# Seven-product column pairs for the head projections of a hybrid encoder step, with attention in a stage of its own

## The chip, the core and the metric

The kernel runs on one core of one Trainium2 chip. The metric is device time in microseconds of one execution. The core has five engines that run side by side and wait for each other through semaphores: TensorE (PE; its weight loads are shown as PEld), VectorE (DVE), ScalarE (ACT), GpSimd (POOL) and SyncE (SP). SP does no arithmetic here: it issues DMAs. ACT and POOL issue some too.

## The reference, cut to what matters

One layer of an encoder is applied to two groups of tokens: 512 tokens of a prompt and 8 x 16 tokens of running streams, 640 rows in all. All numbers are float32.

```python
h = rms_norm(x, g_pre)                       # (640, 2048)
parts = split(h @ w_in)                      # (2048, 13312): heads and gates
o_sb = stick_breaking(q, k, v)               # 6 heads of 128, causal
o_bd = band_attention(q, k, v, rel_bias)     # 6 heads, softmax, bias on distance
o_mm = memory_attention(q, mem_k, mem_v)     # 4 heads, 256 memory tokens
merged = sum(sigmoid(merge_gate) * ((o * silu(g)) @ w_up) for the three branches)
y = x + rms_norm(merged @ w_out, g_post)
```

The columns of `w_in` in blocks of 128: queries, keys, values and SiLU gates of the 6 stick-breaking and the 6 band heads (48 blocks), queries and gates of the 4 memory heads (8 blocks), and three merge gates of 2048 columns (48 blocks). The stream tokens attend to cached keys and values of 512 past tokens (256 for memory) in DRAM as well. New keys and values are outputs.

## The kernel before, in words

Everything is held with features on the partitions and the 640 tokens along a row, in two halves of 320. Each float32 operand is split into a high and a low part of a type that TensorE multiplies faster (`split`, L95 to L97: ACT rounds the high part, DVE subtracts to get the low one), and a product is three matmuls: high by high, high by low, low by high. `load_w` (L120) loads a block of weights as `wr` (SP) and `parts_of` (L107) makes `wh` and `wl`.

A **plain block** (`proj`, L152 to L163) is one block of 128 columns: 16 slabs of 128 features x 3 products x 2 halves of tokens = 96 matmuls of 128x320.

A **pair** (`gate_pair`, L674 to L724) takes two blocks of columns at once. It cuts weights and activations into quadrants (two blocks of columns by two halves of the features; two halves of the features by two halves of the tokens) and forms the result of eight quadrant products out of seven, after Strassen and Winograd. Each product is 8 slabs x 3 matmuls, so a pair is 168 matmuls. The weight sums s1 to s4 are made on POOL for each pair. The activation sums t1 to t4 are made once, on DVE and ACT (`sums`, `whole`, `minus`, L616 to L656); t3 is written over b12, a quadrant of the activations.

The order of the program:

1. Memory keys and values, and the normalised activations `xq` (L176 to L278).
2. Twelve causal heads (`causal_head`, L550), stick-breaking and band in turn. Each runs four plain blocks (gate, value, query, key), then the attention of the prompt (`causal_prompt`) and of the streams (`sample_att`), interleaved step by step. Prompt and stream part share one `b` and one `e` buffer.
3. Four memory heads (`mem_head`), each with two plain blocks; then the first four merge gates, plain (`FIRST`, L38), and the sums.
4. The other 44 merge gates as 22 pairs (L726). Each gate is stored to DRAM (`sig_d`) after its sigmoid.
5. `up` (L750): the gated head outputs, read back from DRAM (`osg_d`), times `w_up`, 48 plain blocks of 6 or 4 slabs, summed under the gates into `merged`.
6. The output projection, norm and residual (L781 on).

Cached keys need a transposition. `load_k` (L471 to L477) reads them from DRAM in pieces of 128 bytes, so that DVE can finish it in 32x32 blocks (L486): four DMAs for each two streams and head, 256 in all. The score matmuls of four streams (L490) are sent one after the other; each uses 32 columns of TensorE's array.

The order within each engine is set by the tile framework: a scheduler takes instructions in program order as their priority, with a timeline of its own, and sends a later one ahead where an earlier one isn't ready. A head's attention thus runs between the matmuls of the next head's plain blocks. The queues of the engines themselves are strictly in order.

Of the kernel before, what the change touches and what calls it, by code (L numbers as in the profile page):

```python
# [43 lines left out]
def stream_step_kernel(  # L44
# [10 lines left out]
    KQ = SP  # L55
# [23 lines left out]
    kv_d = dpool.tile([NMEM, 1024], F32, name="kv_d")  # L79
    osg_d = [dpool.tile([P, NT], F32, name=f"osg_d{i}") for i in range(16)]  # L80
    sig_d = [dpool.tile([P, NT], F32, name=f"sig_d{i}") for i in range(3 * KB)]
# [197 lines left out]


    br = ExitStack()
    stg = br.enter_context(tc.tile_pool(name="stg", bufs=3))
# [28 lines left out]
    def head_q(w, col, need_new=True):  # L311
        acc = new_acc()
        proj(w_in, col, KB, x_src, acc)
        qh = pa.tile([P, TP], F32R, tag="qh", name="qh", bufs=B["q"])
        ql = pa.tile([P, TP], F32R, tag="ql", name="ql", bufs=B["q"])
        for d, c in ((slice(0, HF), acc[:, 0, :HF]), (slice(HF, TP), acc[:, 1, :TP - HF])):
            split(qh[:, d], ql[:, d], c)
        qs = acc[:, 1, HF - P:HF]
        qr = None
        if need_new:  # L320
            qr = pa.tile([P, P], F32, tag="qr", name="qr")
            ACT.copy(qr, qs)
        DVE.tensor_copy(masked(qm, 0), qs.rearrange("p (j a i) -> p j a i", j=4, a=2))
        return qh, ql, qr

    def natural_new(src, outs, name):

        ns = pa.tile([P, P], F32, tag=name + "T", name=name + "T")
        POOL.tensor_copy(ns.rearrange("p (a j i) -> p a j i", a=2, i=TS), stream_order(src[:, TP:]))
        new = pa.tile([P, P], F32, tag=name, name=name)  # L330
        t1 = bank("t1")
        PE.transpose(t1[:, :P], ns, ident)
        ACT.copy(new, t1[:, :P])
        POOL.dma_start(outs, new)
        return new, ns

    def head_k(col, outp, outs):
        acc = new_acc()
        proj(w_in, col, KB, x_src, acc)
        kr = pa.tile([P, NT], F32, tag="rawT", name="kr", bufs=B["raw"])  # L340
        ACT.copy(halves(kr), acc[:, :, :HF])
        kh = pa.tile([P, TP], F32R, tag="kh", name="kh", bufs=B["k"])
        kl = pa.tile([P, TP], F32R, tag="kl", name="kl", bufs=B["k"])
        split(kh, kl, kr[:, :TP])

        nat = pa.tile([P, TP], F32, tag="nat", name="natk")
        DVE.transpose(nat, kr[:, :TP])
        for a in range(4):
            KQ.dma_start(outp[:, 32 * a:32 * a + 32].rearrange("(c i) j -> i c j", i=32),
                         nat[32 * a:32 * a + 32].rearrange("p (c j) -> p c j", j=32))  # L350
        _, kn = natural_new(kr, outs, "kn")
        return kn, kh, kl

    def head_v(col, outp, outs):
        acc = new_acc()
        proj(w_in, col, KB, x_src, acc)
        vt = pa.tile([P, NT], F32, tag="rawT", name="vt", bufs=B["raw"])
        ACT.copy(halves(vt), acc[:, :, :HF])
        nat = pa.tile([P, 4, P], F32, tag="nat", name="nat")
        t0 = bank("t0")  # L360
        for t in range(4):
            PE.transpose(t0[:, t * P:(t + 1) * P], vt[:, t * P:(t + 1) * P], ident)
        DVE.tensor_copy(nat, t0.rearrange("p (t n) -> p t n", t=4))
        POOL.dma_start(outp.rearrange("(t p) e -> p t e", p=P), nat)
        vn, _ = natural_new(vt, outs, "vn")
        vh = pa.tile([P, 4, P], F32R, tag="vh", name="vh", bufs=B["v"])
        vl = pa.tile([P, 4, P], F32R, tag="vl", name="vl", bufs=B["v"])
        split(vh, vl, nat)
        return vn, vh, vl

    def head_g(col):
        acc = new_acc()
        proj(w_in, col, KB, x_src, acc)
        sg = pa.tile([P, NT], F32, tag="sg", name="sg", bufs=B["sg"])
        ACT.activation(halves(sg), acc[:, :, :HF], AF.Sigmoid)
        DVE.tensor_tensor(halves(sg), acc[:, :, :HF], halves(sg), op=ALU.mult)
        return sg

    def w_tiles():
        return (pa.tile([P, 1024], F32R, tag="wth", name="wth", bufs=B["wt"]), pa.tile([P, 1024], F32R, tag="wtl", name="wtl", bufs=B["wt"]))  # L380

    def causal_prompt(q, k, v, sg, kind, strip):

        qh, ql, kh, kl, vh, vl = *q, *k, *v
        for pair in (1, 0):
            nkb = 2 * pair + 2
            wth, wtl = (t.rearrange("p (k n) -> p k n", n=256) for t in w_tiles())
            POOL.memset(wth[:, nkb - 1, 0:P].bitcast(F32), 0.0)
            POOL.memset(wtl[:, nkb - 1, 0:P].bitcast(F32), 0.0)
            for ql_ in (1, 0):  # L390
# [6 lines left out]
                b = pa.tile([P, NT], F32, tag="b", name="b", bufs=B["b"])  # L397
                if kind == "sb":
                    e = pa.tile([P, NT], F32, tag="e", name="e", bufs=B["e"])
# [40 lines left out]
    def mem_prompt_att(q, k, v, sg):  # L440
        qh, ql, kh, kl, vh, vl = *q, *k, *v
        wth, wtl = (t.rearrange("p (k n) -> p k n", n=512) for t in w_tiles())
# [17 lines left out]
    def sample_att(ck, cv, qr, kr, vn, sg, kind, strips):  # L460
        nkb = ck.shape[1] // P
# [9 lines left out]
        def load_k(b):  # L471

            t = pa.tile([P, 2 * nc_ // 32, 32], F32, tag="kc", name="kc", bufs=B["kc"])
            for a in range(4):
                SP.dma_start(t[32 * a:32 * a + 32],
                             ck[b:b + 2, :, 32 * a:32 * a + 32].rearrange("b (c j) i -> j (b c) i", j=32))
            return t.rearrange("p c i -> p (c i)")  # L477

        s = bank("s")
        for par in range(2):  # L480
            kts = []
            for j in range(0, 4, 2):
                kc = load_k(4 * par + j)
                for h in range(2):
                    kt = pa.tile([P, nc_], F32, tag="kt", name="kt", bufs=B["kt"])
                    DVE.transpose(kt, kc[:, h * nc_:(h + 1) * nc_])  # L486
                    kts.append(kt)
                    yield
            for j in range(4):
                PE.matmul(s[32 * j:32 * j + 32, :nc_], qm[:, j, par * 32:par * 32 + 32], kts[j],  # L490
                          start=par == 0, stop=par == 1, tile_position=(0, 32 * j))
            yield
        b = pa.tile([P, NT if new else nc_], F32, tag="b", name="b", bufs=B["b"])
        if new:
            s2 = bank("s2")
            PE.matmul(s2[:, :P], qr, kr, start=True, stop=True)
        if kind == "sb":
            e = pa.tile([P, NT], F32, tag="e", name="e", bufs=B["e"])
# [15 lines left out]
        tp = bank("tp")  # L514
# [3 lines left out]
        o = bank("o")  # L518
        if new:
            t2 = bank("t2")  # L520
# [19 lines left out]
        t3 = bank("t3")  # L540
# [3 lines left out]
    def spill(osg, i):  # L544
        POOL.dma_start(osg_d[i], osg)

    def tokens(t):
# [313 lines left out]
```

## Time and profile before

| | |
|---|---|
| median of 3 runs | 2223.4 us (2222.37 to 2224.03) |
| profiled execution | 2225.07 us, its span 2223.4 us |
| mean granted clock of TensorE | 0.984 |
| stage of the heads and first gates | 95 to 1183 us |
| stage of the gate pairs | 1183 to 1749 us |
| `up` | 1749 to 1985 us |
| output projection | 1985 to 2223 us |

A profile line names the source line (L162), the engine, the operation, the output and inputs by the program's names (`acc<-xh,wh`), the shape and the count (x1920); after the bar stand busy time in us, mean duration in ns, and the idle time of that engine just before, with what ended it. A wait reads "A <- B": A waited for B. "wr<-in_w_in_dram" is a DMA, "SPq" its issue on SP. In the table by stage each engine has its busy time and, in brackets, its count of instructions; then come the granted clock, the busy share of the 16 DMA engines and GB/s.

### The profile page before, as it was taken

How to read it: one execution, taken by the hardware profiler on the slowest of the kernel's cores; microseconds unless marked ns; L12 is line 12 of the kernel's file. 1: busy time of each engine (PE TensorE's matmuls, PEld its weight loads, DVE VectorE, ACT ScalarE, POOL GpSimd, SP SyncE). 2: the span in 40 equal slices, each digit the busy share in tenths (PEclk: the TensorE clock that was granted, in tenths of full speed). 3: DMA queues.
4: the chain of work that ended last, by engine and by line, in shares of the span. 5: the costliest groups of instructions: out<-in, count | busy, mean ns of one | idle time of the engine just before them, and what ended most of it. 6: DMA issues, size and time to landing. Idle time of an engine off the chain costs nothing.

```text
span 2223.4 us, 36183 instructions
## 1 busy us (share of the span) xinstructions
PE 2147.6 (97%) x14277; PEld 1992.9 (90%) x14277; DVE 1074.8 (48%) x1795; ACT 789.0 (35%) x1484; POOL 423.1 (19%) x443
## 2 busy tenths in 40 slices
PE   6999999999999999999997999999999999999997
PEld 4899899898988999978986999999999899998886
DVE  7624444444444444438438555555555434582224
ACT  6422333333323333224344444444444312232221
POOL 3100010000100100000003444544544002340000
PEclk8999999999999999999999999999999999999998
DMA  7665556555564646525442433343333545443224
GB/s 232 181 152 117 133 130 150 128 129 138 146 148 99 155 130 151 144 71 132 124 109 71 132 117 100 104 131 115 100 107 113 161 143 167 145 152 110 76 85 161
DMA packets 574006, 288.55 MB, mean 130 GB/s; under 512 B 277488, under 2 KB 537600, under 8 KB 572812
## 3 DMA queue, kind: packets, MB, share of 16 engines
q1 hardware_dynamic: 560748, 253.18, 43.1%
q10 hardware_dynamic: 9216, 19.93, 2.3%
q0 software_dynamic: 3872, 13.13, 1.7%
q8 instruction: 112, 1.84, 0.3%
q14 instruction: 58, 0.48, 0.1%
HBM read 249.97 MB, written 36.19 MB: 129 GB/s over the span
## 4 chain that ended last, share of the span: by engine, by line
PE 75%; issue 13%; DVE 5%; DMA 3%; POOL 2%; SPq 1%; ACT 1%; ACTq 0%; DVEq 0%; POOLq 0%
PE acc L162 33%; PE q L687 23%; PE ya L148 3%; PE ya L150 3%; PE ya L149 3%; PE s L490 3%; DVE wl L97 2%; POOL merged L764 1%; PE o L535 1%; DMA sig<-sig_d 1%; DMA st<-rext_d 1%; PE tp L413 1%; PE acc L149 0%; PE o L149 0%; DVE yt L828 0%
## 5 line engine op out<-in xcount | busy, mean ns | idle before, releaser
L97 DVE TENSOR_TENSOR wl<-wr,wh 128x512 fp32r<-128x512 f32 (+1 forms) x548 | 411.2, 753 | 621.6 <-ACT wh L96 618.6
L96 ACT CAST wh<-wr 128x512 fp32r<-128x512 f32 (+1 forms) x548 | 330.5, 607 | 806.8 <-PE acc L162 463.6
L162 PE MATMUL acc<-xl,wh 128*128 128x320 f32 x1920 | 453.7, 312 | 0.0
L162 PE MATMUL acc<-xh,wh 128*128 128x320 f32 x1920 | 447.5, 312 | 4.7 <-ACT sig L633 2.5
L162 PE MATMUL acc<-xh,wl 128*128 128x320 f32 x1920 | 450.5, 312 | 0.0
L162 PEld LDWEIGHTS acc<-xh,wh 128*128 128x128 f32 x1920 | 323.8, 189 | 25.0 <-issue 18.6
L162 PEld LDWEIGHTS acc<-xh,wl 128*128 128x128 f32 x1920 | 324.3, 189 | 18.0 <-issue 18.0
L162 PEld LDWEIGHTS acc<-xl,wh 128*128 128x128 f32 x1920 | 325.8, 189 | 15.4 <-issue 14.7
L687 PE MATMUL q<-xh,wh 128*128 128x320 f32 x704 | 218.3, 311 | 5.1 <-ACT wh L96 5.1
L97 DVE TENSOR_TENSOR wl<-ws,wh 128x512 fp32r<-128x512 f32 x176 | 154.6, 879 | 140.1 <-ACT wh L96 139.9
L687 PE MATMUL q<-xh,wl 128*128 128x320 f32 x704 | 214.8, 310 | 5.8 <-DVE wl L97 5.8
L687 PE MATMUL q<-xl,wh 128*128 128x320 f32 x704 | 218.0, 310 | 0.0
L687 PE MATMUL q<-th,wh 128*128 128x320 f32 x528 | 163.2, 309 | 0.7 <-DVE sig L697 0.7
L687 PE MATMUL q<-th,wl 128*128 128x320 f32 x528 | 163.2, 309 | 0.0
L687 PE MATMUL q<-tl,wh 128*128 128x320 f32 x528 | 163.1, 309 | 0.0
L96 ACT CAST wh<-ws 128x512 fp32r<-128x512 f32 x176 | 109.1, 621 | 151.8 <-PE q L687 151.8
L687 PEld LDWEIGHTS q<-xh,wh 128*128 128x128 f32 x704 | 133.1, 189 | 5.6 <-ACT wh L96 5.6
L687 PEld LDWEIGHTS q<-xh,wl 128*128 128x128 f32 x704 | 132.0, 189 | 6.7 <-DVE wl L97 6.7
L687 PEld LDWEIGHTS q<-xl,wh 128*128 128x128 f32 x704 | 133.1, 189 | 0.0
L148 PE MATMUL ya<-wh,gh 128*128 128x512 f32 x320 | 126.6, 396 | 1.0 <-DVE sig L763 1.0
L150 PE MATMUL ya<-wh,gl 128*128 128x512 f32 x320 | 126.6, 395 | 0.0
L149 PE MATMUL ya<-wl,gh 128*128 128x512 f32 x320 | 126.6, 395 | 0.0
(204 smaller groups left out, 3100.9 us busy)
## 6 DMA issues: line engine op xcount, KB each, us to landing
wr<-in_w_in_dram SPq DMA_DIRECT2D x208, 512.0 KB, 4.5
wr<-in_w_out_dram SPq DMA_DIRECT2D x32, 512.0 KB, 3.7
sig_d<-sig ACTq DMA_DIRECT2D x48, 320.0 KB, 3.4
sig<-sig_d SPq DMA_DIRECT2D x48, 320.0 KB, 3.4
kc<-in_cache_sb_k_dram SPq DMA_DIRECT2D x96, 128.0 KB, 3.2
vc<-in_cache_sb_v_dram SPq DMA_DIRECT2D x48, 256.0 KB, 5.8
kc<-in_cache_band_k_dram SPq DMA_DIRECT2D x96, 128.0 KB, 3.2
vc<-in_cache_band_v_dram SPq DMA_DIRECT2D x48, 256.0 KB, 5.1
```

What stands on the lines that cost most here:

```text
L96: ACT.copy(hi, src)
L97: DVE.tensor_tensor(lo, src, hi.bitcast(F32), op=ALU.subtract)
L148: PE.matmul(out, ah, bh, start=start, stop=False)
L149: PE.matmul(out, ah, bl, start=False, stop=False)
L150: PE.matmul(out, al, bh, start=False, stop=stop)
L162: PE.matmul(acc[:, s, :HF], a[:, k], b[s], start=first and f, stop=last and l)
L413: PE.transpose(tp[:, kb * P:(kb + 1) * P], b[:, kb * P:(kb + 1) * P], ident)
L490: PE.matmul(s[32 * j:32 * j + 32, :nc_], qm[:, j, par * 32:par * 32 + 32], kts[j], start=par == 0, stop=par == 1, tile_position=(0, 32 * j))
L535: PE.matmul(o[32 * j:32 * j + 32, :P], l, r, start=i == 0, stop=i == len(steps) - 1, tile_position=(0, 32 * j))
L687: PE.matmul(bank_, a[:, k], b[:, k], start=first and k == 0 and n == 0, stop=k == KH - 1 and n == 2, skip_group_check=not first)
L764: POOL.tensor_tensor(merged[:, j], merged[:, j], sig, op=ALU.add)
```

## The change

All 56 head blocks become 28 pairs. They run, with ten pairs of merge gates, in a stage ahead of attention, and their results go to DRAM: SiLU gates to `sg_d`, queries, keys and values to `q_d`, `k_d`, `v_d` as high and low parts with the stream columns beside them. Four merge gates stay plain at the start (`FIRST`), with the sums beside them. Attention is a later stage: each head loads its parts from DRAM; a head's stream part is interleaved with the next head's prompt part; and 24 merge gates (`LAST`) are plain blocks beside it, traced behind the head of each round, so with a lower priority than that head and a higher one than the next. The quadrant b12 is kept in DRAM and loaded again before that stage.

The cached keys are rearranged by DMAs from DRAM to DRAM (`cut_keys`), 256 of 128-byte pieces, seven behind the weight loads of each pair on SP. Attention then loads them whole, one DMA for each stream. The score matmuls go out two by two, with three `kt` buffers instead of four, six `vc` buffers instead of eight, two `b` and two `e` buffers for the prompt, and `bs` and `es` of its own for the stream part. PSUM is divided anew: eight banks for the pairs; three for late gates, two for stream parts and three for prompt parts in attention.

In `up`, one more buffer holds head outputs, and the split of `merged` is traced within the third branch.

```diff
-B = dict(wr=3, wh=4, wl=4, kc=2, kt=4, vc=8, sg=3, b=1, e=1, raw=1, q=1, k=1, v=1, wt=1)
+B = dict(wr=3, wh=4, wl=4, kc=3, kt=3, vc=6, sg=3, b=2, q=2, v=1, wt=1, nat=1)
 FIRST = 4
+LAST = 24
...
+    def sums(k):
+        r = stg.tile([P, NT], F32, tag="o", name="r")
+        r0, r1 = r[:, :HF], r[:, HF:]
+        r2 = flat()[:, :HF]
+        whole(b11, k, r0), whole(b12, k, r1), whole(b22, k, r2)
+        minus(t1, k, r1, r0)
+        minus(t2, k, r2, r0)
+        minus(t4, k, whole(b21, k, r1), r0)
+    for i in range(FIRST):
+        gate(i)
+        for k in range(KH * i // FIRST, KH * (i + 1) // FIRST):
+            sums(k)
+    def sums3():
+        for k in range(KH):
+            r = stg.tile([P, NT], F32, tag="o", name="r")
+            minus(t3, k, whole(b22, k, r[:, :HF]), whole(b12, k, r[:, HF:]))
...
     def load_quads(col):
...
+        with tc.issue_after(last.ins if hasattr(last, "ins") else last):
+            cut_keys(7)
...
+    def two_parts(o, to):
+        h = flat()
+        split(h.bitcast(F32R), o.bitcast(F32R), o)
+        ACT.dma_start(to[0], h)
+        SP.dma_start(to[1], o)
...
+    class Keys(Queries):
+        def done(self, o, q):
+            nat = flat()
+            DVE.transpose(nat, o[:, :TP])
+            for a in range(4):
+                SP.dma_start(self.outp[:, 32 * a:32 * a + 32].rearrange("(c i) j -> i c j", i=32),
+                             nat[32 * a:32 * a + 32].rearrange("p (c j) -> p c j", j=32))
+            ns, _ = natural_new(o, self.outs)
+            ACT.dma_start(self.to[2], ns)
+            two_parts(o[:, :TP], self.to)
...
+    def cut_keys(n):
+        for to, src, a in cuts[:n]:
+            SP.dma_start(to[32 * a:32 * a + 32].rearrange("p (c i) -> p c i", i=32),
+                         src[:, :, 32 * a:32 * a + 32].rearrange("b (c j) i -> j (b c) i", j=32))
+        del cuts[:n]
...
+    for n, job in enumerate(jobs):
+        block_pair(*job, *([sums3] if n == 0 else []))
+    gs.close()
+    psb.close()
+    for t, d in zip(b12, b12_d):
+        SP.dma_start(t.bitcast(F32), d)
...
-            for j in range(0, 4, 2):
-                kc = load_k(4 * par + j)
-                for h in range(2):
+            for j0 in range(0, 4, 2):
+                kts = []
+                for j in (j0, j0 + 1):
+                    st = 4 * par + j
+                    kc = pa.tile([P, nc_], F32, tag="kc", name="kc", bufs=B["kc"])
+                    SP.dma_start(kc, kx[st // 2][:, st % 2 * nc_:(st % 2 + 1) * nc_])
                     kt = pa.tile([P, nc_], F32, tag="kt", name="kt", bufs=B["kt"])
-                    DVE.transpose(kt, kc[:, h * nc_:(h + 1) * nc_])
+                    DVE.transpose(kt, kc)
                     kts.append(kt)
-                    yield
-            for j in range(4):
-                PE.matmul(s[32 * j:32 * j + 32, :nc_], qm[:, j, par * 32:par * 32 + 32], kts[j],
-                          start=par == 0, stop=par == 1, tile_position=(0, 32 * j))
-            yield
+                for j, kt in zip((j0, j0 + 1), kts):
+                    PE.matmul(s[32 * j:32 * j + 32, :nc_], qm[:, j, par * 32:par * 32 + 32], kt,
+                              start=par == 0, stop=par == 1, tile_position=(0, 32 * j))
+                yield
...
+    heads = [("mm", h) for h in range(4)] + [("sb", h) for h in range(6)] + [("bd", h) for h in range(6)]
     with tc.tile_pool(name="att", bufs=1, reuse_waits="tile") as pa:
         qm, wTm = zero_padded(4)
...
+        before = ()
+        for i, (kind, h) in enumerate(heads + [(None, None)]):
+            mark = last_on_pe()
+            now = mem_head(h) if kind == "mm" else causal_head(h + 6 * (kind == "bd")) if kind else ()
+            interleave(*now[:1], *before)
+            before = now[1:]
+            with tc.issue_after(mark):
+                for n in range(LAST * i // 17, LAST * (i + 1) // 17):
+                    late_gate(3 * KB - LAST + n)
```

`block_pair` is `gate_pair` for any pair of columns: its ends are objects (`Gate`, `Silu`, `Queries`, `Keys`, `Values`) that finish the two results and store them. `late_gate` is `gate` with the two halves of tokens in banks of their own, the second half of the features first.

More of the change, by code (lines that the diff above doesn't have):

```diff
@@ L326, in natural_new @@
[L326 to L369, printed above, removed]
@@ L767, in stream_step_kernel @@
         up(i)
[L768 to L770 removed]
+        if i >= 2 * KB:
+            j = i % KB
+            split(gh[:, j], gl[:, j], merged[:, j])
     br.close()
[L772 removed]
+    psd.close()
     py = ctx.enter_context(tc.tile_pool(name="py", bufs=1, reuse_waits="tile"))
```

438 lines of the change are left out of this document (253 added, 185 removed).

## The prediction

> **What bounds the kernel now.** I read the page's busy times first.
>
> ```profile
> span 2223.4 us, 36183 instructions
> PE 2147.6 (97%) x14277; PEld 1992.9 (90%) x14277; DVE 1074.8 (48%) x1795; ACT 789.0 (35%) x1484; POOL 423.1 (19%) x443
> PE 75%; issue 13%; DVE 5%; DMA 3%; POOL 2%; SPq 1%; ACT 1%; ACTq 0%; DVEq 0%; POOLq 0%
> PE acc L162 33%; PE q L687 23%; PE ya L148 3%; PE ya L150 3%; PE ya L149 3%; PE s L490 3%; DVE wl L97 2%; POOL merged L764 1%; PE o L535 1%; DMA sig<-sig_d 1%; DMA st<-rext_d 1%; PE tp L413 1%; PE acc L149 0%; PE o L149 0%; DVE yt L828 0%
> ```
>
> TensorE is busy for 97% of the span, the next engine for 48%. The chain that ended last (rows three and four) is 75% PE and 13% issue, over half of it projections (L162 plain, L687 in pairs). So the time is a count of matmuls times their pace, plus the places where PE waits. Busy time by stage, cut where the first matmul of each stage starts, says where those are.
>
> ```profile
> core 0: us, PE busy (x) PEld busy (x) DVE busy (x) ACT busy (x) POOL busy (x), PEclk, DMA share, GB/s
> 0.00:95.00 95.00, 68.17 (x304) 53.74 (x305) 73.44 (x125) 55.11 (x100) 27.58 (x19) 0.87 0.64 205
> 95.00:1183.00 1088.00, 1074.92 (x7742) 984.27 (x7740) 491.49 (x965) 361.95 (x707) 71.90 (x207) 0.99 0.54 131
> 1183.00:1749.00 566.00, 549.53 (x3740) 546.12 (x3739) 309.56 (x413) 256.28 (x461) 259.58 (x177) 0.99 0.34 110
> 1749.00:1985.00 236.00, 230.73 (x1536) 228.10 (x1536) 124.57 (x158) 63.14 (x110) 58.14 (x31) 0.99 0.54 163
> 1985.00:2223.40 238.40, 224.22 (x960) 180.65 (x960) 75.72 (x138) 52.56 (x107) 5.90 (x9) 0.98 0.35 111
> ```
>
> The second row is the heads (56 plain blocks, all attention, four gates), the third the 22 gate pairs. PE is idle for 1088.0 - 1074.9 = 13.1 us in the one and 566.0 - 549.5 = 16.5 us in the other: 29.6 us. Busy isn't pace, so the pace comes from a stretch of pairs and from successive rows of a plain block in the timeline.
>
> ```profile
> 1300.00:1700.00 400.00, 400.00 (x2729) 400.00 (x2728) 212.38 (x276) 181.52 (x324) 185.36 (x128) 1.00 0.36 115
> 309.27 0.45 PE L162 MATMUL acc<-xh,wh 128*128 128x320 f32 x2
> 309.56 0.46 PE L162 MATMUL acc<-xl,wh 128*128 128x320 f32 x2
> 309.86 0.46 PE L162 MATMUL acc<-xh,wl 128*128 128x320 f32 x2
> ```
>
> 2729 matmuls in 400 us is 0.1466 us each, so a pair of 168 takes 24.6 us. Plain rows hold two and start 0.29 or 0.30 us apart: the same pace. A pair saves only by its count: two plain blocks are 192 matmuls. The 60 plain blocks of the head stage are 60 x 96 x 0.1466 = 844 us. Of its 1088 us, 244 us are left: 13 idle, 231 for attention's matmuls and transposes.
>
> **The change part by part.** *Products.* The heads' 56 blocks become 28 pairs, four gates stay plain, ten gate pairs remain, and 24 gates go back from pairs to plain blocks. Pairs rise from 22 to 38, plain blocks fall from 60 to 28: 16 x 24 = 384 matmuls fewer, **-56.3 us**. With the two old stages their idle time goes, **-29.6 us**; what stands in its place is costed now.
>
> *First four gates with the sums.* They are 56.3 us of PE. Beside them run the sums of eight slabs, ten DVE instructions each, priced by the first row here, and 16 weight subtractions by the second.
>
> ```profile
> L619 DVE TENSOR_TENSOR r<-xh,xl 128x320 f32<-128x320 f32 x41 | 19.3, 482 | 0.3
> L97 DVE TENSOR_TENSOR wl<-wr,wh 128x512 fp32r<-128x512 f32 x239 | 165.2, 692 | 330.8 <-ACT wh L96 329.8 <-PE acc L162 0.9
> L97 DVE TENSOR_TENSOR wl<-ws,wh 128x512 fp32r<-128x512 f32 x129 | 113.3, 878 | 107.5 <-ACT wh L96 107.3
> 1190.46 4.65 DMA osg_d<-sg
> or<-osg_d SPq DMA_DIRECT2D x16, 320.0 KB, 3.4
> ```
>
> 80 x 0.482 + 16 x 0.692 = 49.7 us: it fits, with 88% of DVE taken. Between 0 and 6 us of waiting; I take 3. *First pair.* The third operand is made in place, in b12, after the last plain gate has read it: 8 x 4 x 0.482 = 15.4 us of DVE, beside ten weight subtractions of the first five products, 8 us by the second and third row. That is 23.5 us against 5 x 24 x 0.1466 = 17.6 us of matmuls: **+6**. Nothing hides the rest, as PE has no other work there.
>
> *Other engines in the pair stage.* A pair now holds 212.4 x 24.6 / 400 = 13.1 us of DVE. A pair of key heads adds two 128x512 transposes and two subtractions, under 3 us by the 692 ns row: 16 of 24.6, still beside matmuls. The value and new-token transposes on PE move here from the head stage; none is added.
>
> *Key caches.* 256 DMAs leave the head stage; 256 DRAM-to-DRAM ones, with both sides in 128-byte pieces, join the pairs, seven behind each pair's last weight load on SP. These are rows on such pieces: the 128-byte reads (kc), 128-byte stores to DRAM (natk), the queue's share in the heads (400 to 900 us), and 5 us with four natk stores.
>
> ```profile
> L475 SPq DMA_DIRECT2D kc<-in_cache_sb_k_dram x96: 311/642/2050, 98.5 to 847.6; - x96
> kc<-in_cache_sb_k_dram SPq DMA_DIRECT2D x96, 128.0 KB, 3.2
> out_dram<-natk SPq DMA_DIRECT2D x48, 64.0 KB, 3.6
> q1 hardware_dynamic: 224127, 62.87, 54.6%
> 232.70:237.70 5.00, 5.00 (x35) 4.86 (x34) 1.95 (x4) 0.89 (x2) 0.54 (x1) 1.00 0.74 170
> DMA packets 3175, 0.85 MB, mean 170 GB/s; under 512 B 2135, under 2 KB 3159, under 8 KB 3175
> ```
>
> SP spends 7 x 0.642 = 4.5 us per pair on issuing. Behind them wait the next pair's weight loads, needed up to 24.6 us later: covered. On the 16 DMA engines a packet of the heads took 0.546 x 500 x 16 / 224127 = 19.5 ns on average. In the last two rows, 0.74 x 5 x 16 us over 2135 small packets is at most 27.7 ns. Nothing in the trace reads and writes such pieces in one transfer, so the cost lies between 0 and the sum of two such packets; I take 19.5 ns, the row with most of them. The 229,376 pieces are then 280 us of the engines' time. The pairs themselves have 0.36 x 936 = 337 us, and the stores of 28 head pairs, about 1.1 MB at 115/0.36 GB/s, 98 us. Together 715 us in a stage of 38 x 24.6 = 936 us: hidden, **0**. The Trainium skill ("DMA: Bandwidth & Descriptors", Specifications) speaks against this: below 512 B the engine does a read-modify-write. The natk row fits that, taking 3.6 us for half the bytes that kc lands in 3.2; a doubling by that rule is the second rival.
>
> *Change into attention.* Its pool takes over the pairs' memory, so head 0's loads wait for the last pair's stores: the last two rows of the fence above the key caches, 4.65 + 3.4 = **+8**, without the first late gate as cover; with it, 0 to 3.
>
> *Attention.* PE has 24 x 96 x 0.1466 = 338 us of gates and 231 us of attention less some 6 us of moved transposes: 563 us, 35 us per head. DVE keeps at most 491.5 - 165.2 = 326 us and gets 96 x 0.692 = 66 for the gates: 393 of 563, not the bound. The cached-key scores go out in twos, no longer in fours:
>
> ```profile
> L490 PE MATMUL s<-kt,qm 128*32 128x512 f32 (+1 forms) x256 | 81.7, 551 | 0.0
> 326.46 1.06 PE L490 MATMUL s<-kt,qm 128*32 128x512 f32 x8
> 972.76 1.05 PE L490 MATMUL s<-kt,qm 128*32 128x512 f32 x4
> 978.25 1.05 PE L490 MATMUL s<-kt,qm 128*32 128x512 f32 x2
> ```
>
> One matmul is two records. One alone takes as long as two or four together, as they share the array. The 82 us now lie between all in fours and all alone. In twos throughout it is about 21 us less; all alone, 34 us more (96 x 1.05 plus 32 half-length ones, less 82). I take **0**, as the present mix already comes from a scheduler that sends each when its key tile is ready. The stage's idle time: the heads' 13.1 us, or 2.5 times it (33) if waiting grows as filler falls from 60 blocks to 24. I take **+20**. Up and output projection stay as they are.
>
> Sum: -56.3 - 29.6 + 3 + 6 + 8 + 20 = **-48.9 us**. The profiled execution took 2225.07 us, 1.7 more than its span; the median of runs equals the span, 2223.4. Forecast: **2174 us**.
>
> **Rivals.** *Attention's own pace sets the end.* A head is a chain of scores, stick or softmax, transposes, values, through four engines. In the trace, the last causal head (its first and last score block, its end) and the last memory head ran with the least beside them:
>
> ```profile
> 953.61 0.48 PE L148 MATMUL s<-kh,qh 128*128 128x512 f32 x1
> 986.65 0.36 PE L148 MATMUL s<-kh,qh 128*128 128x256 f32 x1
> 999.68 0.47 PE L541 MATMUL t<-ident,on 128*128 128x128 f32 x1 [0.39 <-ACT on L538]
> 1152.71 0.28 PE L148 MATMUL s<-kh,qh 128*128 128x256 f32 x1
> 1189.51 0.33 PE L541 MATMUL t<-ident,on 128*128 128x128 f32 x1 [0.41 <-ACT on L538]
> 986.60:1000.40 13.80, 10.00 (x105) 7.81 (x103) 5.32 (x16) 4.17 (x10) 0.00 (x0) 0.75 0.28 71
> ```
>
> 46.1 us and 36.8 us. If nothing overlaps, 12 x 46.1 + 4 x 36.8 = 700 us instead of 583: 2291, slower than before. It decides from (583 + 49)/16 = 39.5 us per head. For it: the granted clock fell to 0.75 where filler was missing. The Trainium skill ("TensorE: Matmul & The Clock Gate", Why this matters for your kernels) has the clock halved after some 3 us of idle PE; the row agrees. Against it: those heads shared one b and one e buffer between prompt and sample part. The change gives the prompt two, the sample its own, and runs a head's sample beside the next head's prompt. The parts are 33 and 13 us, so the longer alone gives 35 or less. 0.09.
>
> *DMA becomes the bound of the pairs.* At twice 19.5 ns the pieces take 559 us, with the rest 994 us against 936: +58, 2232, slower. It decides from 35 ns. For it the natk row; against it that reading and writing of one piece may overlap. 0.05.
>
> *The gates are used up early.* They rank ahead of later heads, so fillers can run out. With five heads left bare, each at half of 46.1 us (two overlapped) instead of the 14 us of PE that it needs: +45, 2219, no change that can be told. It decides when filler is spent at twice the even rate. 0.06.
>
> **How the numbers follow.** The forecast has 0.80. Its own range: without attention's waiting and with scores in twos (-20 - 21), and nothing at first gates, first pair and changeover except 3 (-14), 2119; with 33 us of waiting and scores alone (+13 + 34), 2221. The range given drops the extreme of the low end, where all bounds fall together, and reaches to the third rival and just past 2223: 2126 to 2226. A measurement of this kernel tells about 0.2%, 4.4 us, from no change. Faster: 0.79 of the forecast and 0.02 of the third rival, 0.81; same: 0.01 + 0.04 = 0.05; slower: the first two rivals, 0.14.
>
> **What would show it.** Right: pairs at 24.6 us each from the second on, 38 of them in about 945 us; a PE chain with few DMA steps in that stage; attention at about 583 us with PE over 95% busy; x2 and x4 score rows mixed as now. Wrong: pairs longer than 25 us with PE waiting for wr loads (second rival); PE idle in attention with ACT, DVE or POOL as releaser and a clock under 0.95 (first); no L162-like gate rows in the last heads (third). The forecast is wrong altogether if attention's PE work isn't near 225 us.

## The result, and the profile after

The changed kernel takes 2287.6 us (median of four runs, 2283.17 to 2292.57) against 2223.7 us for the kernel before in the same session: a ratio of 1.028, interval 1.0253 to 1.0311. It is slower by 64 us, where 49 us less had been forecast. The profiled execution took 2292.57 us, with a mean granted clock of 0.975. Busy times and the chain that ended last, from the page of the changed kernel:

```profile
span 2290.9 us, 36585 instructions
PE 2144.2 (94%) x13893; PEld 1950.5 (85%) x13893; DVE 1241.3 (54%) x1919; ACT 862.9 (38%) x1641; POOL 613.3 (27%) x533
PE 78%; DMA 10%; DVE 6%; issue 2%; ACT 2%; SPq 1%; ACTq 0%; POOL 0%; DVEq 0%; POOLq 0%
PE qa L470 19%; PE g L829 14%; PE acc L167 12%; PE qc L470 9%; PE qb L470 4%; DVE wl L102 3%; PE s L710 3%; PE ya L155 3%; PE ya L153 3%; PE ya L154 3%; PE o L755 2%; DMA kc<-kx 2%; DMA wr<-in_w_in_dram 2%; DMA out_dram<-nat 1%; ACT wh L101 1%
```

The matmuls did go: 14277 - 13893 = 384 fewer, as counted. Yet PE's busy time fell by only 3.4 us: those that were left took longer in sum, at a mean granted clock of 0.975 where it was 0.984, and PE's share of the span fell from 97% to 94%. In the chain DMA has grown to 10% (3% before); the line in which DVE makes the low part of the weights (L102, before L97) has 3%, where it had 2%. The table by stage (before the first gates, first gates with sums, pairs, attention, `up`, output projection) shows where:

```profile
0.00:95.00 95.00, 67.46 (x302) 52.94 (x303) 73.25 (x124) 54.71 (x100) 27.50 (x19) 0.93 0.67 213
95.00:152.00 57.00, 57.00 (x389) 56.82 (x388) 42.62 (x78) 21.50 (x41) 10.10 (x8) 1.00 0.62 193
152.00:1176.00 1024.00, 973.58 (x6462) 954.17 (x6462) 623.41 (x782) 438.31 (x819) 467.54 (x326) 0.99 0.57 148
1176.00:1820.00 644.00, 593.94 (x4250) 479.05 (x4249) 299.86 (x640) 232.12 (x466) 43.52 (x139) 0.95 0.67 208
1820.00:2055.00 235.00, 230.74 (x1549) 229.18 (x1550) 128.13 (x160) 63.64 (x111) 60.25 (x33) 0.99 0.53 161
2055.00:2290.90 235.90, 221.46 (x950) 178.35 (x948) 74.05 (x137) 52.60 (x107) 4.37 (x9) 0.98 0.35 112
```

The forecast had 936 + 6 us for the pairs and 8 + 583 for attention. They took 1024 and 644: 82 and 53 us more. The last two stages took 471 us against 474 before. PE was idle for 50 us in each of the two new stages, where 26 had been allowed in both together.

**The pairs.** Pace shows best in a count of the products' matmuls alone. Below are those of the source line that issues them, in a stretch of causal heads (320 to 920 us) and one of gate pairs (980 to 1120 us). Columns: PE and PEld busy with counts, granted clock, DMA share, GB/s.

```profile
320.00:920.00 600.00, 557.78 (x3678) 543.99 (x3679) 0.99 0.63 159
980.00:1120.00 140.00, 139.67 (x949) 138.96 (x948) 1.00 0.55 138
```

With 168 matmuls in a pair, 600 x 168 / 3678 = 27.4 us in the heads and 140 x 168 / 949 = 24.8 us in the gates. So the pace forecast, 24.6, holds for gate pairs, with cache pieces beside them, and fails by some 2.7 us on average for the pairs of the causal heads. It isn't every kind of result: the last two of the four pairs of the memory heads, which end in SiLU gates and queries but have no keys or values, took 49.9 us together (217.8 to 267.7 us). In the timeline, the 24 pairs of the causal heads and the pair behind them, in which the last one's results are finished, ran from 267.7 to 951.8 us: 684 us instead of 616, **+68**. The waits from 320 to 950 us, each with its total, how often, and its longest:

```profile
DVE wl L102 <- ACT wh L101: 148.8, 154, 4.7
DVE o L102 <- DMA out_dram<-o: 56.7, 11, 6.6
ACT nat L101 <- DMA out_dram<-nat: 19.4, 8, 4.0
PEld qa L470 <- DVE wl L102: 18.5, 21, 1.8
PEld qa L470 <- ACT wh L101: 14.6, 13, 2.2
PEld t L452 <- ACT o L413: 7.2, 6, 1.5
PEld tn L427 <- POOL ns L425: 5.6, 12, 1.1
```

Read from the bottom up. PE waits for parts of the weights (rows four and five) and for its own transposes of results (six and seven). DVE, which makes the weights' low parts, has stood up to 6.6 us at `o`: the low part of a result is written over `o`, and must wait until the store of `o` to the output has landed. ACT, which makes the high parts, stands in the same way at `nat`, a single buffer. DVE has 16.5 us of work in each of these pairs (380.2 us from 320 to 950 us, in 630 / 27.4 = 23 pairs), close to the 16 forecast for pairs of keys. It isn't short of time; its queue is in order, and weight parts stand behind a result's store. The first row isn't a sign of loss: the same wait is longer in the faster runs e1 and e7 (253 and 262 us). Three rows of the timeline, behind one pair of keys, show both engines held: ACT behind a store, DVE until ACT's first cast in that row was done (the view names a load that landed in the same moment), and then DVE by a store (in brackets the idle time before, and what ended it):

```profile
482.93 1.14 ACT L101 CAST wh<-wr 128x512 fp32r<-128x512 f32 x2 [3.70 <-DMA out_dram<-new]
483.58 1.29 DVE L102 TENSOR_TENSOR wl<-wr,wh 128x512 fp32r<-128x512 f32 x2 [3.63 <-DMA wr<-in_w_in_dram]
490.94 0.71 DVE L440 STREAM_TRANSPOSE nat<-o 128x512 f32<-128x512 f32 x1 [2.57 <-DMA kh_d<-nat]
```

**The first pair** (the first 168 matmuls of the products) took 40.7 us, 16 over 24.6, where 6 had been allowed; its clock fell to 0.83. **Attention** falls into a part while late gates last, and a bare end:

```profile
1176.00:1714.00 538.00, 531.11 (x3774) 440.57 (x3773) 254.87 (x532) 210.66 (x413) 38.35 (x121) 0.99 0.69 214
1714.00:1820.00 106.00, 62.83 (x476) 38.47 (x476) 44.98 (x108) 21.46 (x54) 5.17 (x18) 0.74 0.57 177
```

While there are gates, 7 us are lost in 538. Then the last three and a half heads run alone, some 30 us each: 43 us idle in 106, and what runs has a granted clock of 0.74. The longest wait of SP's queue there, for a buffer of cached values (L695) held by the value matmuls (L755):

```profile
SPq L695 <- PE o L755: 25.1, 7, 15.1
```

### The profile page after: what moved, and what is told of

The parts are those of the page before. It is cut to its first block, busy times and chain, and to the rows that moved or that the text cites. A ratio compares the mean times of both kernels' runs of the same rounds, so it can differ in the third digit from the quotient of the medians.

```text
span 2290.9 us, 36585 instructions
## 1 busy us (share of the span) xinstructions
PE 2144.2 (94%) x13893; PEld 1950.5 (85%) x13893; DVE 1241.3 (54%) x1919; ACT 862.9 (38%) x1641; POOL 613.3 (27%) x533
## 4 chain that ended last, share of the span: by engine, by line
PE 78%; DMA 10%; DVE 6%; issue 2%; ACT 2%; SPq 1%; ACTq 0%; POOL 0%; DVEq 0%; POOLq 0%
PE qa L470 19%; PE g L829 14%; PE acc L167 12%; PE qc L470 9%; PE qb L470 4%; DVE wl L102 3%; PE s L710 3%; PE ya L155 3%; PE ya L153 3%; PE ya L154 3%; PE o L755 2%; DMA kc<-kx 2%; DMA wr<-in_w_in_dram 2%; DMA out_dram<-nat 1%; ACT wh L101 1%
## 5 line engine op out<-in xcount | busy, mean ns | idle before, releaser
L102 DVE TENSOR_TENSOR wl<-wr,wh 128x512 fp32r<-128x512 f32 (+1 forms) x516 | 395.5, 771 | 430.1 <-ACT wh L101 418.6
L102 DVE TENSOR_TENSOR wl<-ws,wh 128x512 fp32r<-128x512 f32 x304 | 317.2, 1058 | 131.1 <-ACT wh L101 129.0
L829 PE MATMUL g<-xh,wl 128*128 128x320 f32 x768 | 242.4, 316 | 0.0
L829 PE MATMUL g<-xl,wh 128*128 128x320 f32 x768 | 242.1, 315 | 0.0
L829 PE MATMUL g<-xh,wh 128*128 128x320 f32 x768 | 241.1, 314 | 0.0
L470 PE MATMUL qa<-xh,wh 128*128 128x320 f32 x608 | 193.6, 318 | 13.7 <-ACT wh L101 9.5
L470 PE MATMUL qa<-xh,wl 128*128 128x320 f32 x608 | 193.5, 318 | 12.2 <-DVE wl L102 11.8
L470 PE MATMUL qa<-th,wh 128*128 128x320 f32 x608 | 189.0, 311 | 7.2 <-DVE o L474 5.7
L463 POOL TENSOR_TENSOR ws<-wr 128x512 f32<-128x512 f32 x114 | 167.8, 1486 | 98.1 <-DVE wl L102 62.0
L470 PE MATMUL qa<-xl,wh 128*128 128x320 f32 x608 | 190.8, 314 | 2.6 <-DVE xl L102 2.6
L470 PE MATMUL qa<-th,wl 128*128 128x320 f32 x608 | 188.2, 309 | 1.8 <-DVE wl L102 1.8
L470 PE MATMUL qa<-tl,wh 128*128 128x320 f32 x608 | 187.8, 309 | 0.0
```

Of the source, the lines that this page charges most:

```text
L102: DVE.tensor_tensor(lo, src, hi.bitcast(F32), op=ALU.subtract)
L463: eng.tensor_tensor(o, a[c], b[c], op=op)
L470: PE.matmul(bank_, a[:, k], b[:, k], start=first and k == 0 and n == 0, stop=k == KH - 1 and n == 2, skip_group_check=not first)
L829: PE.matmul(acc[s], a[:, k], b[s], start=(k0, k, n) == (8, 0, 0), stop=(k0, k, n) == (0, 7, 2))
```

## The experiments

The texts on record give the theories letters. A: the store of each result in two parts holds DVE and ACT up, and weight parts behind them. B: the cache pieces slow the landings. C: late gates are sent too early and leave the last heads bare. D: heads have a pace of their own, and gates beside them are free. E: the lost time is the place of a pair's end work in the queues, whether it waits for landings or not. G: SP's queue stands at buffers and keeps loads back. Medians go against the kernel before on the same chip, 2226.0 to 2228.3 us. Where no interval is given, the kernel ran once.

**e1_raw** stores each result whole and splits it after loading, in attention (A).

```diff
     def two_parts(o, to):
-        h = flat()
-        split(h.bitcast(F32R), o.bitcast(F32R), o)
-        ACT.dma_start(to[0], h)
         SP.dma_start(to[1], o)
...
-        for to, src in zip(t, d):
+        for to, src in list(zip(t, d))[1:]:
             SP.dma_start(to.bitcast(F32), src)
+        split(t[0], t[1], t[1].bitcast(F32))
```

> Queries, keys and values go to DRAM whole, and each head splits them when it loads them in the attention stage; nothing is split, and nothing is overwritten in place, at the end of a head pair. Theory A (DVE and ACT stand in order behind the landings of result stores, with the weight parts of the next products queued behind them): the head pairs fall from about 27.3 us to 25.3 or less, 25 of them, so the pair stage loses 50 us or more; attention gains 33 us of DVE work spread over 642 us and stays within 10 us; total about 2240. Theory B (the key-cache pieces crowd the weight loads out of the DMA engines): the pairs stay at about 27, total within 10 us of 2288.

It took 2257.4 us, ratio 1.014 (1.0125 to 1.0155). The products' matmuls from 320 to 920 us:

```profile
320.00:920.00 600.00, 571.53 (x3820) 562.21 (x3820) 1.00 0.60 149
```

That is 26.4 us per pair: 1.0 us of the 2.7, neither A's 25.3 nor B's 27. DVE's wait at `o` is gone, and PE's waits for weight parts are down from 33 us to 10.5; those at the transposes of new tokens have grown from 5.6 to 10.4. The waits for landings that are left lie at other results (PE's rows first):

```profile
PEld qa L467 <- DVE wl L102: 5.3, 10, 1.0
PEld qa L467 <- ACT wh L101: 5.2, 8, 1.0
PEld tn L424 <- POOL ns L422: 10.4, 12, 2.1
POOL ns L422 <- DMA ks_d<-ns: 33.8, 6, 6.2
ACT wh L101 <- PE tn L424: 30.9, 6, 5.7
```

POOL now stands at the new tokens' buffer, PE's transpose waits for POOL, and ACT, which is to copy its result, has a weight part queued behind it. A is right in kind and a third of the size.

**e2_nocuts** leaves the rearrangement of the caches out (B); attention loads plain rows instead.

```diff
-        with tc.issue_after(last.ins if hasattr(last, "ins") else last):
-            cut_keys(7)
...
-                    SP.dma_start(kc, kx[st // 2][:, st % 2 * nc_:(st % 2 + 1) * nc_])
+                    SP.dma_start(kc, kx(st, nc_))
```

> The rearranging DMAs are left out; attention loads rows of the same size from the caches as they lie, so its cached keys are not the right ones and the cached scores are meaningless. Theory B (key-cache pieces crowd out the weight loads): head pairs fall from 27.3 us to about 24.6, total about 2220. Theory A (in-order waits for landings of result stores): head pairs stay between 26.5 and 27.5, total within 20 us of 2288.

It took 2260.7 us. The same stretch, and the wait at `o`:

```profile
320.00:920.00 600.00, 577.19 (x3869) 567.83 (x3869) 1.00 0.44 135
DVE o L102 <- DMA out_dram<-o: 39.1, 9, 6.2
```

26.1 us per pair, 1.3 better, with a shorter wait at the same place. So the copies, costed at 0, cost about a microsecond in each head pair, though the DMA engines were busy for 63% of that stretch, and next to nothing in gate pairs, which store little. They did not crowd out the weight loads, as B had it: those landed in 5.2 us at the median with the copies and without. Most stores landed sooner without them (those of `o` to the output in 4.4 us for 4.8, of `nat` in 3.0 for 4.1), two of ACT's later (`qh_d` and `vh_d`).

**e8_raw_nocuts** does both.

> Parts stored whole, and the rearranging DMAs left out as well (cached keys not the right ones). Each of the two alone took 0.9 and 1.2 us off a head pair of 27.3. If they are two ways into the same loss (a queue waits for a store to land, and landings take longer beside the key-cache pieces), both together give little more than the better one: about 25.8. If they are separate losses they add up: about 25.2, and the rest is PE's own waiting for transposes.

It took 2257.0 us, as e1 alone:

```profile
320.00:920.00 600.00, 572.10 (x3838) 563.25 (x3838) 1.00 0.39 116
```

26.3 us per pair. A and B don't add: with the parts' stores gone the copies cost nothing (26.4 with, 26.3 without). They are two handles on one loss: copies lengthen the landings at which DVE and ACT stand, as most of the medians above have it. The copies also hold SP's queue, 0.757 us each at the median, with stores behind them; the runs don't part this from the longer landings.

**e5_defer** traces the whole end of a pair (transposes, splits, stores) behind the second product of the next pair.

```diff
-        e0.done(o0, SP)
...
-        e1.done(o1, ACT)
+        late_ends.extend([lambda: e0.done(o0, SP), lambda: e1.done(o1, ACT)])
...
         product(qb, a12, b21, True)
         add(o0[:, LO], qb)
+        finish()
```

> The end work of a pair (transposes, splits, stores of its two results) is traced behind the second product of the next pair instead of at the end of its own, so that it comes after that pair's first weight parts and PE meets its transposes when their inputs are long there. Nothing else changes. Theory E (the lost time is the end work's place in the in-order queues of PE, ACT and DVE): head pairs fall from 27.3 us to 25.3 or less, pair stage about 970, total about 2235. Theory A in its first form (only the waits for store landings count, wherever the end work stands): DVE still stops for each landing with weight parts behind it, pairs stay at 26.5 or more, total 2270 or more.

It took 2278.8 us, ratio 1.0235 (1.0218 to 1.0252), at 26.8 us per pair:

```profile
320.00:920.00 600.00, 571.78 (x3757) 561.84 (x3756) 0.98 0.64 163
```

PE's waits at its transposes are gone; that was about 0.6 us a pair. The waits for weight parts moved with the end work, as A had it and not E: pairs now alternate between 24.6 to 25.0 us (behind SiLU gates and queries) and 27 to 31 (behind values and keys).

**e3_pin** holds each round's late gates back until the previous round's attention (C).

```diff
-        before = ()
+        before, mark = (), last_on_pe()
         for i, (kind, h) in enumerate(heads + [(None, None)]):
-            mark = last_on_pe()
...
             before = now[1:]
+            done = last_on_pe()
             with tc.issue_after(mark):
...
+            mark = done
```

> Each late gate's matmuls are kept behind the attention of the round before the one in which it is traced, so that gates can't run ahead of their round. Theory C (gates are used up by 1714 us and three and a half heads run bare): PE's idle time in the attention stage falls from about 50 us to 20, the stage from 650 to about 620, total about 2257. Theory D (a head's own chain of four engines sets the stage's pace): the stage stays at 650 or gets longer, total 2288 or more.

It took 2301.4 us, ratio 1.035 (1.0321 to 1.0381), worse by 14 us. The idle time moved from the bare end into the rounds with gates, and did not shrink. **e6_gates_last** does the opposite: all late gates are traced behind all heads, so that they only fill.

```diff
-            with tc.issue_after(mark):
-                for n in range(LAST * i // 17, LAST * (i + 1) // 17):
-                    late_gate(3 * KB - LAST + n)
+            if i == 0:
+                first = mark
+        with tc.issue_after(first):
+            for n in range(LAST):
+                late_gate(3 * KB - LAST + n)
```

> All 24 late gates are traced behind all heads, so that attention has the higher priority throughout and gates only fill its holes. Theory C (bare heads cost the time; heads themselves can go at some 25 us): attention is over after about 420 us, the rest of the gates runs dense, stage about 595 instead of 645, total about 2238. Theory D (a head's chain takes 37 us or more whatever is beside it): 16 x 37 = 592 us with the gates spent within it, and the end bare: stage 630 or more, total 2270 or more.

It took 2293.8 us, ratio 1.031 (1.0281 to 1.0334). The gates were still used up 109 us before the end, with 42 us of PE's idle time behind the last one. **e4_last34** gives attention ten more gates, so that five pairs fewer run.

```diff
-LAST = 24
+LAST = 34
...
-            cut_keys(7)
+            cut_keys(8)
```

> 34 instead of 24 gates are plain blocks beside attention, so five pairs fewer; eight instead of seven cache pieces per pair. Theory C (heads run bare when the gates are used up; a head with gates beside it runs at the pace of PE): the pairs lose 5 x 24.6 = 123 us, the attention stage gains 10 x 14.1 = 141 us of matmuls and loses up to 45 us of idle time, total about 2261. Theory D (the chain sets the pace, gates fill its holes for nothing): the attention stage stays at 650, total about 2165.

It took 2261.7 us. The attention stages of the three, in the columns of the table by stage, first e3:

```profile
1170.00:1826.00 656.00, 603.60 (x4255) 479.92 (x4253) 300.81 (x641) 225.10 (x462) 40.64 (x140) 0.95 0.67 205
```

then e6:

```profile
1181.00:1830.00 649.00, 596.09 (x4253) 481.16 (x4251) 300.96 (x640) 224.35 (x460) 42.88 (x139) 0.95 0.67 207
```

and e4:

```profile
1049.00:1789.00 740.00, 723.19 (x5212) 609.80 (x5212) 324.92 (x681) 268.76 (x529) 41.52 (x140) 0.99 0.65 200
```

Idle are 52, 53 and 17 us. So the gates' order isn't the cause (C falls in that form; e3 and e6 came out as D had them). But e4 came out where C had it, at 2261, and gates aren't free (D falls: ten more cost 96 us of the stage, for 10 x 14.1 = 141 us of matmuls). The heads lack filler: while there is some PE stays busy, and each gate moved here fills a part of the 50 us. Each pair given up for it costs two plain gates less one pair, 28.1 - 24.6 = 3.5 us.

**e7_all** puts e1, e5 and e6 together.

> Parts stored whole and split in attention, end work behind the next pair's second product, late gates behind all heads. If A, E and C each hold a part: pair stage about 955, attention about 600, total about 2180, below the kernel before (2224). If the parts only move the waits elsewhere: 2230 or more.

A miss: 2243.2 us, ratio 1.0076 (1.006 to 1.0091), where 2180 had been expected. Products and waits in the heads:

```profile
320.00:920.00 600.00, 581.97 (x3890) 573.51 (x3889) 0.99 0.63 155
```

```profile
PEld qa L467 <- DVE wl L102: 10.1, 11, 1.4
PEld qa L467 <- ACT wh L101: 8.7, 9, 1.3
```

25.9 us per pair: half of the loss is gone, and PE's waits for weight parts are about halved (19 us for 33), though e1 alone had 10.5. 1.3 us a pair stay, and four pairs in a row show where (behind keys, SiLU gates, values and queries):

```profile
472.30:500.80 28.50, 26.99 (x171) 26.26 (x170) 0.94 0.67 146
500.80:525.40 24.60, 24.60 (x170) 24.60 (x169) 1.00 0.61 157
525.40:552.80 27.40, 25.50 (x170) 24.63 (x169) 1.00 0.63 158
552.80:577.50 24.70, 24.70 (x171) 24.70 (x170) 1.00 0.60 154
```

The end work of SiLU gates and queries is now hidden; the loss that is left lies behind values and keys, whose end work has transposes, new tokens and stores to the outputs as well. Attention took 634 us with 43 idle, 10 less than in the changed kernel.

**e9_bias_pool** issues the loads of the bias strips from POOL instead of SP (G).

```diff
-            SP.dma_start(strip, ext_ap(h, 0, [[1, P], [1, 512]]))
+            POOL.dma_start(strip, ext_ap(h, 0, [[1, P], [1, 512]]))
```

(and two such lines more)

> The 17 loads of the band heads' bias (strip, st) are issued by POOL instead of SP; nothing else changes. Theory G (in the bare heads SP's queue is the bound: 42 loads for a band head, some of them standing in a wait with the next head's loads behind them): without 17 of them the bare end with its 44 us of idle PE shrinks by 15 us or more, total about 2270. Theory D (the chain through PE, ACT and DVE sets a bare head's time): unchanged within 5 us.

It went the other way: 2303.9 us, 16 us more than the changed kernel's median and 11 more than its slowest run. **e10_vc8** gives the cached values eight buffers again, and takes one from the stream results.

```diff
-B = dict(wr=3, wh=4, wl=4, kc=3, kt=3, vc=6, sg=3, ...
+B = dict(wr=3, wh=4, wl=4, kc=3, kt=3, vc=8, sg=2, ...
```

> Eight vc buffers instead of six (and two sg buffers instead of three, to make room), as many as the streams of a head, so that SP no longer stands in the seventh and eighth value load until PE has used the first ones. Theory G: SP's waits for PE at the value loads (25 us between 1714 and 1820, one of 15 us) go, the idle time of the bare end falls from 44 to 25 us or less, total about 2268. Theory D: unchanged within 5 us.

It took 2273.6 us. Attention in e9:

```profile
1175.00:1831.00 656.00, 594.67 (x4253) 479.09 (x4251) 300.09 (x640) 233.25 (x466) 91.99 (x233) 0.96 0.71 207
```

and in e10, with its bare end:

```profile
1173.00:1798.00 625.00, 580.13 (x4254) 475.71 (x4252) 300.40 (x640) 227.29 (x462) 40.76 (x139) 0.96 0.68 215
1724.00:1798.00 74.00, 43.19 (x351) 26.45 (x347) 33.10 (x79) 17.20 (x41) 2.84 (x9) 0.75 0.53 170
```

The stage is 19 us shorter than in the changed kernel's profiled run, the slowest of its four; by the times, the two buffers are worth 14 us against the median and 10 against the fastest. SP had stood up to 15 us at one value buffer, with the next heads' loads behind it, and its 25.1 us at these buffers are down to 8.4. G holds in part for this wait, and not for the bias loads. In e9 POOL's busy time in the stage doubled, from 44 to 92 us; that this made it slower is argued, not shown. In e10's bare end 31 us of 74 are still idle, where G had 25 or less: the same share as before, in a shorter end.

**e11_best** takes e1, e5, `LAST = 32`, `cut_keys(8)` and e9's bias loads; **e12_best_vc8** adds e10's buffers; **e13_no_bias** is e12 with the bias loads on SP again.

> Parts stored whole, end work behind the next pair's second product, 32 late gates (8 cache pieces per pair), bias loads on POOL. Added up from the runs so far (pair stage at 25.7 us per head pair as with the first two together, attention's idle time at 20 as with 34 gates): about 2215, just below the kernel before (2224 to 2228). If filler and end work compete for the same waits: 2235.

> As the run before, with eight vc and two sg buffers. Theory G: 5 to 15 us faster than that run. Theory D: the same within 4 us.

> As the run before (parts stored whole, end work behind the next pair's second product, 32 late gates, eight vc and two sg buffers), but with the bias loads on SP again. If POOL's part in the bias loads costs what it did alone (16 us there, where it put them into POOL's queue ahead of attention's own work): 5 to 15 us faster, about 2210. If that difference was only the schedule's luck: the same as before within 4 us, about 2221.

They took 2236.9 us (1.005, interval 1.0034 to 1.0067), 2221.1 us (0.9975, 0.9963 to 0.9987) and **2216.4 us (0.9955, 0.9941 to 0.9969)**. The attention stage of e12:

```profile
1046.00:1750.00 704.00, 687.47 (x5020) 580.00 (x5020) 344.33 (x713) 287.41 (x560) 91.90 (x234) 0.99 0.67 193
```

and of e13:

```profile
1048.00:1743.00 695.00, 687.59 (x5020) 579.81 (x5020) 343.52 (x712) 284.15 (x557) 43.55 (x140) 1.00 0.63 193
```

e11 came out at its second value, 2235. The value buffers are worth 16 us here too. The bias loads on SP give 5 us more, at the edge of what can be told: the intervals of e12 and e13 overlap. In e13 attention has 7 us of idle time left and a full clock. This version beats both kernels, the one before by 10 us or 0.45%, though its pairs still take more than 24.6 us.

**e14_no_sums3** never makes t3, to size the first pair.

```diff
-        block_pair(*job, *([sums3] if n == 0 else []))
+        block_pair(*job)
```

> The kernel after the change with the third operand never made: b12 itself stands in its place, so all results of pairs are wrong; everything else as it was. If the first pair's 16 us beyond the others are that operand's DVE and ACT work: the first pair falls from 40.7 to 26 us or less. If they are the stage's start (banks, weights, sums still running): it stays above 35.

It took 2281.5 us. The products' matmuls of the first pair in the changed kernel:

```profile
152.10:192.80 40.70, 30.83 (x168) 28.41 (x168) 0.83 0.29 79
```

and in e14:

```profile
153.50:181.40 27.90, 25.17 (x169) 24.64 (x169) 1.00 0.34 84
```

t3 costs 12.8 us of the 16; the other 3 are left to the start. 27.9 us lies between the two values expected, close to the first.

## Why the prediction was wrong

The profiled spans are 2223.4 and 2290.9 us. Against the forecast of 2174.5 by the sum, 116 us are to be found: pairs +82, attention +53, first gates -2, `up` and output -4, and -13 for work that the forecast's sum holds but its stages leave out: 6 us of transposes that move to the pairs, and 7.5 of attention's end in the old pair stage.

*Right.* The products: 384 matmuls fewer, gate pairs at 24.8 us. First gates with sums: 57.0 us for 59.3. The change into attention: the late gate covered it. Up and output projection: unchanged.

*Other engines in the pair stage* is the step that failed first, +68, of which 6 are the moved transposes' own time. It said "16 of 24.6, still beside matmuls" and priced the end of a pair at 0. The 16 us were right. The inference was not: room in an engine's total is no cover when its queue is in order and holds a landing ahead of the next weights. The forecast itself asked what is queued behind each wait only for SP; DVE, ACT and POOL each got a wait for a store, and the next product's weights stood behind. The changed kernel's waits, e1 and e5 show it, and e7 shows half of the loss removed by moving or dropping that work. The other half, 1.3 us a pair in e7, lies behind values and keys; which part of their end work costs it stays open. One candidate was DVE's subtraction of weight sums, which took 1058 ns, where the row of before has 878:

```profile
L102 DVE TENSOR_TENSOR wl<-ws,wh 128x512 fp32r<-128x512 f32 x304 | 317.2, 1058 | 131.1 <-ACT wh L101 129.0
```

In e7 it falls: there the subtraction took 831 ns in the pair of 27.4 us shown above and 933 ns in the pair of 24.7 us behind it.

*Key caches*, 0, hid the same mistake. The engines' share stayed near 0.63, under the 0.76 that the forecast's own sum gives, so the second rival (DMA as the bound) did not happen. The copies cost 1.3 us a pair by holding up stores, and only where an engine stood at a landing (e2 against e8).

*First pair*, +6, measured 16. The sum took DVE's work less the matmuls beside it. t3 isn't needed at the end of those five products, but made in the same queue as their weight parts; e14 gives it 12.8 us.

*Attention*, 563 busy + 20 idle, came to 594 + 50. Filler did not run short evenly, as the factor 2.5 had it: nearly all of the idle time lies in the 106 us after the last gate. That is the third rival in size, 43 us for its 45, though the gates were spent at only 1.2 times the even rate (over 538 of 644 us), not twice. The stage comes to 644 / 16 = 40.3 us per head, just past the 39.5 from which the first rival decides, but not by that rival's 700 us in series: two heads did overlap, at some 30 us each when alone. Of the 31 us of busy time too many, by an estimate 62.8 x 0.26 = 16 come from the granted clock of 0.74 in the bare end and 7.5 from an end of attention that the forecast had left in the old pair stage. The cached-key scores, taken at 0, cost 9 more, 90.7 us for 81.7 before; some of that is the same clock, so the three come to about the 31:

```profile
L710 PE MATMUL s<-kt,qm 128*32 128x512 f32 (+1 forms) x256 | 90.7, 579 | 16.2 <-DVE sm L664 9.4 <-DVE kt L707 4.7 <-DMA kc<-kx 2.1
```

The Trainium skill ("TensorE: Matmul & The Clock Gate", Why this matters for your kernels) has the clock fall to half behind a gap of some 3 us without matmuls. Here the trace agrees in kind: in the bare end, with waits of PE of up to 10.8 us, the clock was 0.74, and 0.99 while gates last. So a wait is paid a second time in the pace behind it.

So an idle time of 30 us was taken away with the old stages and 100 us put in its place. In the kernel before, 60 plain blocks stood beside all of attention and hid all but 13 us of the waits of its chain; the price of taking them away was the term that the forecast bounded too low.

## What to carry to other kernels

A busy share says what an engine could do, not when: for each operation added to an in-order queue, ask what it waits for (a store that must land before its buffer is written again, above all) and what stands behind it. Work that fills the gaps of a chain of short steps is worth more than its own time; count how much of it the chain needs before moving it out. When a saving and its cost lie in different stages, tune the border between them: eight more plain gates and two more buffers, with the results stored whole and finished later, turned 64 us of loss into 10 of gain.

## What the runs showed of the hardware

Copies within DRAM in pieces of 128 bytes were cheaper than forecast. In the stretch from 320 to 920 us they move 148,480 pieces (139 copies of 1024 and 12 of 512), and the DMA share is 0.63 with them and 0.44 without: 0.19 x 600 x 16 / 148,480 = 12.3 ns a piece, or 13.7 if the share without is scaled to as many pairs; 19.5 had been taken. Their landing, at the median:

```profile
kx<-in_cache_sb_k_dram SPq DMA_DIRECT2D x96, 128.0 KB, 4.4
```

4.4 us, where the same pieces read into the core's memory before landed in 3.2. The Trainium skill's read-modify-write below 512 bytes ("DMA: Bandwidth & Descriptors", Specifications) would have made it twice the forecast price by the prediction's reading; no run here shows that.

A subtraction of weight parts on DVE (128x512, both inputs in the core's memory) goes slower beside POOL. From 320 to 920 us those of weight sums took 684 ns on average where no POOL instruction ran beside them, and 1526 ns where one of POOL's sums ran all along (in e7 687 and 951; in the kernel before, from 1300 to 1700 us, 692 and 918). Two rows of the changed kernel's timeline, the first beside POOL's sums, the second without:

```profile
469.26 1.52 DVE L102 TENSOR_TENSOR wl<-ws,wh 128x512 fp32r<-128x512 f32 x1 [0.46 <-ACT wh L101]
491.57 0.65 DVE L102 TENSOR_TENSOR wl<-ws,wh 128x512 fp32r<-128x512 f32 x1
```
